# An encoder trunk on one core: boundary products doubled for six blocks instead of eight, a weight split moved behind the first gate, and the differential logits of a head in one burst

## The chip, the cores and the metric

One core of a Trainium2 chip runs the kernel. TensorE (PE) does the matmuls and transposes into PSUM, which has eight banks of 128 partitions; VectorE (DVE), ScalarE (ACT) and GpSimd (POOL) do the elementwise work; SyncE (SP) issues the loads of weights. The metric is the device time of one execution in microseconds; the kernel before takes 1092.3 us, the median of three runs.

## The reference, cut to what matters

A sequence of 16 meta tokens and 256 tokens (T = 272, D = 1024) goes through two layers. Each layer is a half-step SwiGLU feed-forward, a token mixer, and a second half-step feed-forward; every one of the six sub-layers has a norm at its input and one at its output. The mixer of layer 0 is a neighbourhood attention on a 4 x 64 grid, that of layer 1 a differential attention with a relative-position bias.

```
h = h + 0.5 * rmsnorm(swiglu(rmsnorm(h, g[0]), gate0, up0, down0), g[1])
h = h + rmsnorm(mixer(rmsnorm(h, g[2])), g[3])
h = h + 0.5 * rmsnorm(swiglu(rmsnorm(h, g[4]), gate1, up1, down1), g[5])
# mixer of layer 1, per head, with two half heads s = 0, 1 of width 64:
logits[s] = (q[s] * 64 ** -0.5) @ k[s].T + bias
a = softmax(logits[0]) - lam * softmax(logits[1])
o = rmsnorm(a @ v, subln_g) * (1 - lambda_init)
```

## The kernel before

**Weights and precision.** All activations are held transposed, 128 features on the partitions and 272 (or 256) tokens along the row, in eight blocks. The weights are 328 units of 1024 x 128, 512 KB each, loaded in order of use by SP into five `raw` buffers. Each value is split into a high and a low part of the type fp32r: `split_hi` (L128) casts half a unit on ACT to `whi`, `split_lo` (L134) subtracts on DVE to `wlo`; two of each make a unit ready, and the second `split_lo` issues the load that goes into the freed raw buffer. A **pump** splits one unit ahead of its use; with `W_BUFS` = 7, up to seven units may be split and not done. A product of one 128 x 128 block is three matmuls (`mm3`, L182 to L184): `whi` by the high part of the input, `wlo` by the high part, `whi` by the low part. A unit is eight blocks, 24 matmuls.

**Banks.** PSUM's eight banks are one `st` for statistics, three named `att`, and four named `acc`. The feed-forwards alternate over the seven (`all_banks`); in the attentions `acc` holds projections and `att` the rest.

**The norms.** The scale of an input norm (`r2`) is not applied to the input but to the product: the input's parts `xhi`, `xlo` are of h times the gain, and `r2` multiplies what comes out of PSUM. `InputRstd.begin` sums squares with single-column matmuls (L247), DVE adds the epsilon (`v`), POOL takes the power, `end` spreads the result over a bank by three transposes (L268), and ACT copies it to `r2` (L305).

**The start.** `start` has seven gate and up units of the first feed-forward: four in a group while the input arrives, then units 4, 5 and 6 one by one. The sums come in unit 5, the transposes ahead of unit 6's first block. Behind the last matmul `pump(4)` splits four units. Then the feed-forward reads the banks: `gt` (L437) and `ut` (L438) on DVE multiply gate and up by `r2`, ACT takes the silu, DVE the product.

**The boundaries.** A sub-layer's output f is added to h only after its own norm, whose scale is known when all eight blocks of f are there. `Post.feed` takes each block off PSUM: the square on ACT (added up on POOL, L278), f on DVE (`fg`), and f times the next gain split into `fhi` and `flo`. At each of the five boundaries between sub-layers `enter` then fills the wait: unit 0 of the next sub-layer is multiplied by the old h (`xhi`, `xlo`) into one bank `ab[0]` and by f (`fhi`, `flo`) into another, `ab[1]`, all eight blocks of both, 48 matmuls. In their midst stand the sums of f's squares (ahead of block `ready`, 6 or 7, of the first product) and the transposes that spread f's scale (ahead of block 2 of the second). `Post.add` scales f, adds it to h (L357) and makes the new `xhi` (L282) and `xlo`. `ab[1]` times the scale plus `ab[0]` is unit 0's result. `proj_group` then takes the next five units block by block, all high parts of a block first, then its low parts, with the sums of the new input norm ahead of block 6 and its transposes ahead of block 7.

**The order.** PE runs in program order everywhere. On DVE, ACT and POOL the feed-forwards run in program order too (`tc.manual_schedule()`); in the attentions a scheduler orders the three. There, a **filler** (`Filler`: the projections of units 6 to 23 and the first three output groups, 165 blocks of three matmuls) is cut into chunks by `pipeline`, and the steps of a head (the differential attention's are `logits`, `weights`, `turn_v`, `turn_a`, `values`, `scale`, `turn_o`) stand at set chunks, eight chunks a head. Pumps stand at three of every eight chunks. In the differential attention `logits` is called twice a head (chunks 2 and 3, one half of the queries each): three matmuls for each of the two half heads, which lie on partitions 0 to 63 and 64 to 127, into two `att` banks; DVE adds the bias and reduces (`tensor_tensor_reduce`), ACT takes exponentials (L1011). `weights` makes A of both half heads (L1019 on ACT, L1020 on DVE), and `turn_a` (chunks 7 and 8) transposes it on PE (L1079).

Of the kernel before, what the change touches and what calls it, by code (L numbers as in the profile page):

```python
# [39 lines left out]
W_BUFS = 7  # L40
# [9 lines left out]
def encoder_kernel(ctx, tc, xT, wall, gT, bqkvT, boT, sublnT, rpbP, metab, lam_p, rel,  # L50
# [20 lines left out]
    def att_tile():  # L71
        return psum.tile([P, 512], F32, tag="att", name=nm("att"), bufs=3)

    def acc_tile():

        pools["turn"] = (pools["turn"] + 1) % 7
        if pools["wide"] and pools["turn"] % 2:
            return att_tile()
        return psum.tile([P, 512], F32, tag="acc", name=nm("acc"), bufs=4)
# [115 lines left out]
    def proj_group(units, n_of, ihi, ilo, accs, hook):  # L195

        ws = [next_unit() for _ in units]
        for k in range(KB):
            if k in hook:
                hook[k]()  # L200
            for j in range(len(units)):
                n = n_of(units[j])
                nc.tensor.matmul(accs[j][:, :n], ws[j][0][:, k, :], ihi[:, k, :n], start=k == 0, stop=False)  # L203
                nc.tensor.matmul(accs[j][:, :n], ws[j][1][:, k, :], ihi[:, k, :n], start=False, stop=False)  # L204
            for j in range(len(units)):
                n = n_of(units[j])
                nc.tensor.matmul(accs[j][:, :n], ws[j][0][:, k, :], ilo[:, k, :n], start=False, stop=k == KB - 1)  # L207
        done(len(units))
# [79 lines left out]
    class InputRstd:  # L288
# [5 lines left out]
        def feed(self, m, engine=nc.gpsimd):  # L294
            sq = square(h[:, m, :self.n], self.n)
            self.acc = sq if m == 0 else add_squares(self.acc, sq, self.n, engine)
# [10 lines left out]
    class Post:  # L307
# [3 lines left out]
        def __init__(self, n, gain, bias, gain_next, n_next, ready):  # L311
            self.n, self.gain, self.bias = n, gain, bias
            self.gain_next, self.n_next, self.ready = gain_next, n_next, ready
            self.acc = None

        def open(self):
            self.cm = tc.tile_pool(name=nm("fx"), bufs=1, side="right")
            pool = self.cm.__enter__()
            self.fhi = pool.tile([P, KB, T], F32R, tag="fhi", name=nm("fhi"))
            self.flo = pool.tile([P, KB, T], F32R, tag="flo", name=nm("flo"))  # L320

        def feed(self, m, ps):
            n = self.n
            f = fg[:, m, :n]
            pump_hi() if m < KB - 1 else None
            if self.bias is None:
                sq = square(ps, n)
                nc.vector.tensor_scalar(out=f, in0=ps, scalar1=self.gain[:, m:m + 1], scalar2=None, op0=ALU.mult)
            else:
                sq = square(ps, n, bias=self.bias[:, m:m + 1])  # L330
                nc.vector.tensor_scalar(out=f, in0=ps, scalar1=self.bias[:, m:m + 1],
                                        scalar2=self.gain[:, m:m + 1], op0=ALU.add, op1=ALU.mult)
            self.acc = sq if m == 0 else add_squares(self.acc, sq, n)
# [29 lines left out]
    def enter(post, n_of, ab, rest):  # L363
# [5 lines left out]
        for k in range(KB):  # L369
            if k == post.ready:  # L370
                post.rstd()
# [828 lines left out]
```

## Time and profile before

| kernel before | us |
|---|---|
| median of three runs (1091.28 to 1093.07) | 1092.3 |
| the profiled execution, whole | 1092.72 |
| its span in the profile | 1090.9 |
| PE busy, share of the span | 99% |
| DVE busy, share of the span | 71% |
| ACT busy, share of the span | 56% |

The span runs from the first to the last instruction that the profiler recorded. Engines are busy side by side, so the shares add up to more than 100%. A wait in brackets behind an instruction, as in "[3.36 <-DVE gt L437]", is the engine's idle time ahead of it and what ended it. PEclk is the share of TensorE's full clock that was granted in a stretch. The matmul records overlap: a matmul's record lasts longer than the distance to the next one's start.

### The profile page before, as it was taken

The numbers are of one execution on the slowest core, as the hardware profiler recorded it, in microseconds if no ns is written. First come the engines' busy times: TensorE is split into PE (matmuls) and PEld (weight loads), VectorE is DVE, ScalarE is ACT, GpSimd is POOL, SyncE is SP. The second block draws the span as 40 slices with busy tenths as digits, with TensorE's granted clock in tenths as the row PEclk, the third lists the DMA queues.
The fourth block names the chain that finished last, engine by engine and source line by source line (L and its number), as shares of the span: only waits on it lengthen the run. The fifth ranks groups of instructions, "written<-read, shape, count | busy, mean of one in ns | idle before, by whom it ended". The sixth has DMA issues, their size and how long they took to land.

```text
span 1090.9 us, 22240 instructions
## 1 busy us (share of the span) xinstructions
PE 1076.9 (99%) x8482; PEld 1053.2 (97%) x8482; DVE 776.1 (71%) x1679; ACT 615.6 (56%) x1414; POOL 134.5 (12%) x259
## 2 busy tenths in 40 slices
PE   9899999999999999999999999999999999999997
PEld 8899999999999999999999999999999999999986
DVE  6876668687777896665578766666887778867642
ACT  6555455467666564445546544554677855655541
POOL 0000001143122260000130000001321131000000
PEclk9999999999999999999999999999999999999999
DMA  8599784615324375796526655555253344755541
GB/s 273 184 152 249 220 232 155 194 59 194 117 98 136 100 230 175 201 233 190 176 61 216 193 185 163 177 184 182 72 180 98 117 136 124 244 182 186 183 166 39
DMA packets 65772, 181.49 MB, mean 166 GB/s; under 512 B 13944, under 2 KB 23672, under 8 KB 65656
## 3 DMA queue, kind: packets, MB, share of 16 engines
q1 hardware_dynamic: 65232, 179.73, 54.4%
q8 instruction: 67, 1.10, 0.4%
q14 instruction: 41, 0.34, 0.1%
q10 hardware_dynamic: 432, 0.33, 0.1%
HBM read 178.91 MB, written 1.20 MB: 165 GB/s over the span
## 4 chain that ended last, share of the span: by engine, by line
PE 91%; DVE 4%; ACT 2%; issue 1%; POOL 0%; DMA 0%; POOLq 0%; ACTq 0%; DVEq 0%
PE acc L182 16%; PE acc L184 15%; PE acc L183 15%; PE att L182 10%; PE att L184 9%; PE att L183 9%; PE acc L204 1%; PE acc L203 1%; PE acc L207 1%; DVE wlo L134 1%; PE acc L513 1%; PE acc L512 1%; PE acc L511 1%; DVE h L357 1%; DVE xlo L285 1%
## 5 line engine op out<-in xcount | busy, mean ns | idle before, releaser
L134 DVE TENSOR_TENSOR wlo<-raw,whi 128x512 fp32r<-128x512 f32 (+2 forms) x668 | 437.2, 694 | 57.1 <-ACT whi L128 54.0
L128 ACT CAST whi<-raw 128x512 fp32r<-128x512 f32 (+2 forms) x668 | 374.9, 607 | 96.8 <-issue 43.5
L182 PE MATMUL acc<-xhi,whi 128*128 128x272 f32 (+1 forms) x1008 | 297.5, 295 | 3.4 <-DVE gt L437 3.4
L184 PE MATMUL acc<-xlo,whi 128*128 128x272 f32 (+1 forms) x1008 | 290.5, 288 | 0.0
L183 PE MATMUL acc<-xhi,wlo 128*128 128x272 f32 (+1 forms) x1008 | 289.6, 287 | 0.0
L182 PEld LDWEIGHTS acc<-xhi,whi 128*128 128x128 f32 x1008 | 190.8, 189 | 7.8 <-issue 6.3
L183 PEld LDWEIGHTS acc<-xhi,wlo 128*128 128x128 f32 x1008 | 190.9, 189 | 0.0
L184 PEld LDWEIGHTS acc<-xlo,whi 128*128 128x128 f32 x1008 | 190.7, 189 | 0.0
L182 PE MATMUL att<-xhi,whi 128*128 128x272 f32 (+1 forms) x552 | 158.8, 288 | 0.0
L184 PE MATMUL att<-xlo,whi 128*128 128x272 f32 (+1 forms) x552 | 158.7, 287 | 0.0
L183 PE MATMUL att<-xhi,wlo 128*128 128x272 f32 (+1 forms) x552 | 158.1, 286 | 0.0
L439 ACT ACTIVATE gt<-gt 128x272 f32<-128x272 f32 (+1 forms) x88 | 37.7, 428 | 142.4 <-DVE gt L437 142.4
L182 PEld LDWEIGHTS att<-xhi,whi 128*128 128x128 f32 x552 | 104.1, 189 | 0.0
L184 PEld LDWEIGHTS att<-xlo,whi 128*128 128x128 f32 x552 | 104.1, 189 | 0.0
L183 PEld LDWEIGHTS att<-xhi,wlo 128*128 128x128 f32 x552 | 104.0, 188 | 0.0
L184 PE MATMUL acc<-mlo,whi 128*128 128x272 f32 x286 | 82.9, 290 | 0.0
L183 PE MATMUL acc<-mhi,wlo 128*128 128x272 f32 x286 | 82.4, 288 | 0.0
L182 PE MATMUL acc<-mhi,whi 128*128 128x272 f32 x286 | 82.1, 287 | 0.0
L443 ACT CAST mhi<-ut 128x272 fp32r<-128x272 f32 (+1 forms) x88 | 36.5, 415 | 66.7 <-DVE ut L441 66.7
L184 PE MATMUL att<-mlo,whi 128*128 128x272 f32 x242 | 70.1, 290 | 0.0
L278 POOL TENSOR_TENSOR sqa<-sqa,sq 128x272 f32<-128x272 f32 (+1 forms) x60 | 50.3, 838 | 159.3 <-ACT sq L273 157.2
L183 PE MATMUL att<-mhi,wlo 128*128 128x272 f32 x242 | 69.7, 288 | 0.0
(241 smaller groups left out, 2018.9 us busy)
## 6 DMA issues: line engine op xcount, KB each, us to landing
raw<-wall SPq DMA_DIRECT2D x324, 512.0 KB, 4.1
bias<-tab SPq DMA_DIRECT2D x8, 320.0 KB, 8.2
raw<-wall SPq DMA_DIRECT2D x16, 128.0 KB, 3.8
bias<-tab SPq DMA_DIRECT2D x8, 256.0 KB, 8.4
h<-xT SPq DMA_DIRECT2D x3, 272.0 KB, 4.2
out<-ht SPq DMA_DIRECT2D x3, 256.0 KB, 2.0
grow<-glast SPq DMA_DIRECT2D x1, 512.0 KB, 5.1
h<-xT ACTq DMA_DIRECT2D x2, 136.0 KB, 4.3
```

Of the source, the lines that this page charges most:

```text
L128: nc.scalar.copy(split[i][0][:, sl], raw[i][:, sl])
L134: nc.vector.tensor_tensor(out=wlo[:, sl], in0=raw[i][:, sl], in1=whi[:, sl].bitcast(F32), op=ALU.subtract)
L182: nc.tensor.matmul(ps, whi_k, mhi, start=first, stop=False)
L183: nc.tensor.matmul(ps, wlo_k, mhi, start=False, stop=False)
L184: nc.tensor.matmul(ps, whi_k, mlo, start=False, stop=last)
L203: nc.tensor.matmul(accs[j][:, :n], ws[j][0][:, k, :], ihi[:, k, :n], start=k == 0, stop=False)
L204: nc.tensor.matmul(accs[j][:, :n], ws[j][1][:, k, :], ihi[:, k, :n], start=False, stop=False)
L207: nc.tensor.matmul(accs[j][:, :n], ws[j][0][:, k, :], ilo[:, k, :n], start=False, stop=k == KB - 1)
L278: engine.tensor_tensor(out=t[:, :n], in0=acc[:, :n], in1=sq[:, :n], op=ALU.add)
L285: nc.vector.scalar_tensor_tensor(out=xlo[:, m, :n], in0=h[:, m, :n], scalar=gain[:, m:m + 1], in1=xhi[:, m, :n].bitcast(F32), op0=ALU.mult ...
L439: nc.scalar.activation(gt[:, :n], gt[:, :n], AF.Silu)
L443: nc.scalar.copy(mhi[:, f, :n], ut[:, :n])
```

## The change

**Boundaries.** Unit 0 is multiplied twice for the first six blocks only (`AHEAD = 6`); its blocks 6 and 7 join `proj_group` and use the new `xhi` and `xlo`, in the bank `ab[0]`. So `fhi` and `flo` have six blocks, the sums of f's squares stand ahead of block 4 of the first product, the last square is added on DVE, and the order in `feed` changes for the last blocks. In `proj_group` the hooks stand behind a block's high parts instead of ahead of them. **Start.** The four pumps behind unit 6 are gone; the transposes stand ahead of block 7 of unit 5 instead of ahead of unit 6, with one pump ahead of them. The pumps in `evac` stay. **Banks and buffers.** Four `att` and three `acc` banks instead of three and four, eight weight buffers instead of seven; the DMA scratch shrinks. **Attentions.** `enter` and the staging of the first six units stand in `manual_schedule`. **Differential attention.** `logits` makes all twelve matmuls of a head at once, into four banks, alternating between the two half heads; chunks and pumps get new numbers, and the fillers are spread by `ahead`.

```diff
-W_BUFS = 7
+W_BUFS = 8
+AHEAD = 6
...
-        return psum.tile([P, 512], F32, tag="att", name=nm("att"), bufs=3)
+        return psum.tile([P, 512], F32, tag="att", name=nm("att"), bufs=4)
...
-        return psum.tile([P, 512], F32, tag="acc", name=nm("acc"), bufs=4)
+        return psum.tile([P, 512], F32, tag="acc", name=nm("acc"), bufs=3)
...
+    def proj_group(units, n_of, ihi, ilo, accs, hook, begun=()):
+        parts = [(w, acc, n, AHEAD) for w, acc, n in begun]
+        parts += [(next_unit(), acc, n_of(u), 0) for u, acc in zip(units, accs)]
         for k in range(KB):
+            here = [p for p in parts if k >= p[3]]
+            for w, acc, n, _ in here:
+                nc.tensor.matmul(acc[:, :n], w[0][:, k, :], ihi[:, k, :n], start=k == 0, stop=False)
+                nc.tensor.matmul(acc[:, :n], w[1][:, k, :], ihi[:, k, :n], start=False, stop=False)
             if k in hook:
                 hook[k]()
...
+            for w, acc, n, _ in here:
+                nc.tensor.matmul(acc[:, :n], w[0][:, k, :], ilo[:, k, :n], start=False, stop=k == KB - 1)
+        done(len(parts))
...
         def feed(self, m, ps):
...
+            if m == KB - 1:
+                self.acc = add_squares(self.acc, sq, n, nc.vector)
...
+            if m >= AHEAD:
+                pump_lo()
+                return
...
         n0 = n_of(0)
         w = next_unit()
-        for k in range(KB):
-            if k == post.ready:
+        for k in range(AHEAD):
+            if k == 4:
                 post.rstd()
-            mm3(ab[0][:, :n0], w[0][:, k, :], w[1][:, k, :], xhi[:, k, :n0], xlo[:, k, :n0], k == 0, k == KB - 1)
-        for k in range(KB):
+            mm3(ab[0][:, :n0], w[0][:, k, :], w[1][:, k, :], xhi[:, k, :n0], xlo[:, k, :n0], k == 0, False)
+        for k in range(AHEAD):
             if k == 2:
                 post.spread()
             mm3(ab[1][:, :n0], w[0][:, k, :], w[1][:, k, :], post.fhi[:, k, :n0], post.flo[:, k, :n0],
-                k == 0, k == KB - 1)
-        done()
+                k == 0, k == AHEAD - 1)
...
+        pump(1)
+        proj_group(range(1, 1 + len(rest)), n_of, xhi, xlo, rest, {6: ir.begin, 7: ir.end}, [(w, ab[0], n0)])
         nc.vector.tensor_tensor(out=u0[:, :n0], in0=ab[0][:, :n0], in1=u0[:, :n0], op=ALU.add)
-        pump(1)
-        proj_group(range(1, 1 + len(rest)), n_of, xhi, xlo, rest, {6: ir.begin, 7: ir.end})
-        pump(1)
         return [u0] + rest, ir
...
         proj_group(range(FIRST), lambda u: n, xhi, xlo, accs, {})
+
+        def end():
+            pump(1)
+            ir.end()
+
         for i in range(FIRST, 7):
-            proj(accs[i], n, xhi, xlo, {5: {2: ir.begin}, 6: {0: ir.end}}.get(i))
-        pump(4)
+            proj(accs[i], n, xhi, xlo, {5: {2: ir.begin, 7: end}}.get(i))
         return accs, ir
...
-            accs = [acc_tile() for _ in range(4)]
+            accs = [acc_tile() for _ in range(3)]
             ab = [att_tile() for _ in range(2)]
-            accs, ir = enter(before, nof, ab, accs + [att_tile()])
+            with tc.manual_schedule():
+                accs, ir = enter(before, nof, ab, accs + [att_tile(), att_tile()])
...
+                ps = [[att_tile() for _ in rows] for _ in range(2)]
+                for qt in range(2):
+                    q = slice(qt * P, (qt + 1) * P)
+                    for i, (a, b) in enumerate(((qhi, khi), (qlo, khi), (qhi, klo))):
+                        for s, r in enumerate(rows):
+                            nc.tensor.matmul(ps[qt][s][:, :T], a[r, q], b[r, :], start=i == 0, stop=i == 2)
...
-            at = [(2, logits, 0), (3, weights, 0), (3, logits, 1), (4, weights, 1), (7, turn_a, 0), (8, turn_a, 1)]
+            at = [(6, weights, 0), (7, weights, 1), (11, turn_a, 0), (12, turn_a, 1)]
             steps = [(c, lambda hh, go=go, qt=qt: go(hh, qt)) for c, go, qt in at]
-            steps += [(6, turn_v), (10, values), (11, scale), (13, turn_o)]
-            pipeline(fl, steps, (0, 5, 6))
+            steps += [(5, logits), (9, turn_v), (14, values), (15, scale), (18, turn_o)]
+            pipeline(fl, steps, (0, 1, 2), ahead=3)
...
-    nc = bacc.Bacc("TRN2", target_bir_lowering=False, num_devices=1)
+    nc = bacc.Bacc("TRN2", target_bir_lowering=False, num_devices=1, dynamic_dma_scratch_size=1024)
```

The changed order is shown at three places. In the rows, a name before the arrow is written, the names behind it are read, and numbers count tiles. First DVE at the first norm: `v` is the epsilon added to the sums, `gt` and `ut` the first gate and up block taken off PSUM. Before:

```order
L255 TENSOR_SCALAR v_404<-st_403 128x3
L134 TENSOR_TENSOR wlo_459<-raw_218,whi_458 128x512 x2
L134 TENSOR_TENSOR wlo_467<-raw_221,whi_466 128x512 x2
L134 TENSOR_TENSOR wlo_475<-raw_229,whi_474 128x512 x2
L134 TENSOR_TENSOR wlo_483<-raw_255,whi_482 128x512 x2
L437 TENSOR_TENSOR gt_498<-acc_135,r_27_432 128x272
L438 TENSOR_TENSOR ut_499<-att_136,r_27_432 128x272
L441 TENSOR_TENSOR ut_499<-gt_498,ut_499 128x272
L134 TENSOR_TENSOR wlo_504<-raw_275,whi_503 128x512 x2
L444 TENSOR_TENSOR mlo_494<-ut_499,mhi_493 128x272
```

And of the changed kernel:

```order
L135 TENSOR_TENSOR wlo_270<-raw_215,whi_269 128x512 x2
L257 TENSOR_SCALAR v_404<-st_403 128x3
L135 TENSOR_TENSOR wlo_427<-raw_218,whi_426 128x512 x2
L452 TENSOR_TENSOR gt_474<-att_135,r_27_437 128x272
L453 TENSOR_TENSOR ut_475<-acc_136,r_27_437 128x272
L456 TENSOR_TENSOR ut_475<-gt_474,ut_475 128x272
L135 TENSOR_TENSOR wlo_480<-raw_221,whi_479 128x512 x2
L459 TENSOR_TENSOR mlo_470<-ut_475,mhi_469 128x272
```

Between `v` and the first `gt` stood eight weight splits, of four units; now two stand there, and the next two come after the product `ut`.

Second, PE at the logits of the first head; `acc` is the filler. Before, the first of its two bursts:

```order
L184 MATMUL acc_10242<-xlo,whi_10153 128x272
L182 MATMUL att_10257<-hi_10187,hi_10181 128x272
L183 MATMUL att_10257<-hi_10187,lo_10182 128x272
L184 MATMUL att_10257<-lo_10188,hi_10181 128x272
L182 MATMUL att_10263<-hi_10187,hi_10181 128x272
L183 MATMUL att_10263<-hi_10187,lo_10182 128x272
L184 MATMUL att_10263<-lo_10188,hi_10181 128x272
L182 MATMUL acc_10242<-xhi,whi_10153 128x272
```

And of the changed kernel, the one burst:

```order
L1034 MATMUL att_10263<-hi_10141,hi_10136 128x272
L1034 MATMUL att_10264<-hi_10141,hi_10136 128x272
L1034 MATMUL att_10263<-hi_10141,lo_10137 128x272
L1034 MATMUL att_10264<-hi_10141,lo_10137 128x272
L1034 MATMUL att_10263<-lo_10142,hi_10136 128x272
L1034 MATMUL att_10264<-lo_10142,hi_10136 128x272
L1034 MATMUL att_10265<-hi_10141,hi_10136 128x272
L1034 MATMUL att_10266<-hi_10141,hi_10136 128x272
L1034 MATMUL att_10265<-hi_10141,lo_10137 128x272
L1034 MATMUL att_10266<-hi_10141,lo_10137 128x272
L1034 MATMUL att_10265<-lo_10142,hi_10136 128x272
L1034 MATMUL att_10266<-lo_10142,hi_10136 128x272
```

The six matmuls that wrote one bank after the other have become twelve that alternate between two banks, and then between the next two.

Third, ACT at the start of the differential attention, from the copy of `r2` on: `hi` are high parts of q and k, L1011 (L1042 in the changed kernel) the first exponentials. Before:

```order
L305 COPY r_712_10136<-st_10110 128x272
L990 CAST hi_10181<-qk_10179 128x256
L128 CAST whi_10238<-raw_9782 128x512 x2
L128 CAST whi_10325<-raw_9812 128x512 x2
L990 CAST hi_10187<-qk_10185 128x272
L128 CAST whi_10346<-raw_9844 128x512 x2
L128 CAST whi_10385<-raw_10018 128x512 x2
L990 CAST hi_10195<-qk_10193 128x256
L128 CAST whi_10492<-raw_10159 128x512
L1011 ACTIVATE L_10253,sm_10256<-L_10253,nmx_10255 128x272 x2
```

And of the changed kernel, where the copy of `r2` and two more `hi` stand ahead of the first row:

```order
L1013 CAST hi_10150<-qk_10148 128x256
L1013 CAST hi_10155<-qk_10153 128x272
L129 CAST whi_10162<-raw_9708 128x512 x2
L1013 CAST hi_10198<-qk_10196 128x256
L129 CAST whi_10202<-raw_9751 128x512 x2
L129 CAST whi_10217<-raw_9778 128x512 x2
L129 CAST whi_10231<-raw_9810 128x512 x2
L129 CAST whi_10329<-raw_9971 128x512 x2
L129 CAST whi_10350<-raw_10168 128x512 x2
L1013 CAST hi_10253<-qk_10251 128x272
L1042 ACTIVATE L_10261,sm_10280<-L_10261,nmx_10279 128x272 x2
L1042 ACTIVATE L_10261,sm_10286<-L_10261,nmx_10285 128x272 x2
```

Of the `whi` casts nine half units stood ahead of the first exponentials; now twelve do, and four casts of q and k stand in a row ahead of them.

## Rows read from the trace of the kernel before

**Rows 1.** The page's busy times: us, share of the span, instructions.

```profile
PE 1076.9 (99%) x8482; PEld 1053.2 (97%) x8482; DVE 776.1 (71%) x1679; ACT 615.6 (56%) x1414; POOL 134.5 (12%) x259
```

**Rows 2.** Windows: length; PE, PEld, DVE, ACT, POOL busy (instructions); clock; DMA; GB/s.

```profile
32.60:36.00 3.40, 3.40 (x15) 3.40 (x16) 3.18 (x7) 2.63 (x6) 0.00 (x0) 0.50 1.02 349
...
36.00:39.40 3.40, 3.40 (x28) 3.40 (x28) 3.18 (x8) 1.79 (x4) 0.00 (x0) 1.00 0.88 313
...
100.00:140.00 40.00, 40.00 (x319) 40.00 (x319) 26.52 (x53) 20.25 (x42) 0.00 (x0) 1.00 0.83 236
...
1000.00:1020.00 20.00, 20.00 (x171) 20.00 (x171) 14.32 (x30) 9.96 (x22) 0.00 (x0) 1.00 0.55 179
```

**Rows 3.** Waits of PE: waiting instruction, releaser: us in total, times, longest.

```profile
PE acc L182 <- DVE gt L437: 3.4, 1, 3.4
...
PE st L247 <- POOL sqa L278: 1.3, 3, 0.6
...
PE att L1079 <- DVE A L1020: 1.0, 1, 1.0
```

**Rows 4.** Timeline at the first norm: start, duration, instruction, [wait, releaser]; PE, ACT, DVE.

```profile
28.87 0.29 PE L184 MATMUL att<-xlo,whi 128*128 128x272 f32 x1
...
32.52 0.53 PE L182 MATMUL acc<-xhi,whi 128*128 128x272 f32 x1 [3.36 <-DVE gt L437]
...
26.18 0.39 ACT L305 COPY r<-st 128x272 f32<-128x272 f32 x1 [4.20 <-PE st L268]
...
27.11 4.90 DVE L134 TENSOR_TENSOR wlo<-raw,whi 128x512 fp32r<-128x512 f32 x8 [3.35 <-ACT whi L128]
...
31.94 0.43 DVE L437 TENSOR_TENSOR gt<-acc,r 128x272 f32<-128x272 f32 x1
```

**Rows 5.** Timeline at the entries of two sub-layers, PE and ACT.

```profile
349.12 0.83 PE L247 MATMUL st<-ones,sqa 128*128 128x1 f32 x6 [0.38 <-POOL sqa L278]
...
351.14 0.54 PE L268 MATMUL st<-ident,r 128*128 128x128 f32 x3
...
352.73 0.53 ACT L282 ACTIVATE xhi<-h,g_sb 128x272 fp32r<-128x272 f32 x1 [3.38 <-DVE h L357]
...
908.76 0.61 PE L247 MATMUL st<-ones,sqa 128*128 128x1 f32 x4 [0.60 <-POOL sqa L278]
```

**Rows 6.** Timeline of PE around two bursts of differential logits.

```profile
782.48 0.29 PE L184 MATMUL acc<-xlo,whi 128*128 128x272 f32 x1
...
783.28 0.39 PE L182 MATMUL acc<-xhi,whi 128*128 128x272 f32 x1
...
783.51 0.29 PE L183 MATMUL acc<-xhi,wlo 128*128 128x272 f32 x1
...
784.01 0.29 PE L184 MATMUL acc<-xlo,whi 128*128 128x272 f32 x1
...
785.07 0.39 PE L182 MATMUL acc<-xhi,whi 128*128 128x272 f32 x1
```

**Rows 7.** Start of the differential attention: timeline (PE, ACT), DMA issues, a window.

```profile
776.84 0.49 PE L268 MATMUL st<-ident,r 128*128 128x128 f32 x3
...
781.18 0.41 ACT L990 CAST hi<-qk 128x272 fp32r<-128x272 f32 x1
...
781.50 2.18 ACT L128 CAST whi<-raw 128x512 fp32r<-128x512 f32 x4
...
784.92 0.51 ACT L1011 ACTIVATE L<-L,nmx 128x272 f32<-128x272 f32 x1
...
788.78 0.28 PE L184 MATMUL acc<-xlo,whi 128*128 128x272 f32 x1
...
790.07 0.44 PE L1079 MATMUL att<-ident,A 128*128 128x128 f32 x2 [1.01 <-DVE A L1020]
...
raw<-wall SPq DMA_DIRECT2D x324, 512.0 KB, 4.1
...
783.00:871.00 88.00, 86.99 (x710) 81.65 (x707) 71.70 (x211) 72.03 (x226) 17.58 (x21) 1.00 0.41 136
```

More of the change, by code (lines that the diff above doesn't have):

```diff
@@ L868, in natten @@
                     single.append((i, lambda p=pairs, go=go: go(p)))
-            for u in range(6):
-                stage(u, accs[u])
-            post = Post(T, gains(l, 3), bo_sb, gain_next, n_next, 7)
+            with tc.manual_schedule():
+                for u in range(6):
+                    stage(u, accs[u])
+                pump(1)
+            post = Post(T, gains(l, 3), bo_sb, gain_next, n_next)
             fl = Filler(range(6, 24), lambda u: T, stage, ohi, olo, post)
@@ L933, in pipeline @@
             want = total * (i + 1) // chunks_all
+            if ahead:
+                even = total * (last + ahead) // chunks_all
+                want = (even * (i + 1) // last if i < last else
+                        even + (total - even) * (i + 1 - last) // (chunks_all - last))
             fl.fill(want - filled)
@@ new lines, in stage_hi, with stage, logits @@
+                return lambda: engine.tensor_tensor(out=lo, in0=s, in1=hi.bitcast(F32), op=ALU.subtract)
+            def stage(u, a):
+                low = stage_hi(u, a)
+                if low is not None:
+                    low()
+            def logits(hh):
+                (qhi, qlo), (khi, klo) = staged[3 * hh], staged[3 * hh + 1]
+                L = cur["L"] = pt.tile([P, 2, 2, T], F32, tag="L", name=nm("L"))
+                cur["A"] = pt.tile([P, 2, T], F32, tag="A", name=nm("A"))
+                rows = [slice(64 * s, 64 * s + 64) for s in range(2)]
+                ps = [[att_tile() for _ in rows] for _ in range(2)]
[4 more added lines that the diff above has]
+                            nc.tensor.matmul(ps[qt][s][:, :T], a[r, q], b[r, :], start=i == 0, stop=i == 2)
+                for qt in range(2):
+                    nmx = pt.tile([P, 2], F32, tag="nmx", name=nm("nmx"))
+                    sm = pt.tile([P, 2], F32, tag="sm", name=nm("sm"))
+                    for s in range(2):
+                        nc.vector.tensor_tensor_reduce(
+                            out=L[:, qt, s, :], in0=ps[qt][s][:, :T], in1=b4[:, hh, qt, :], scale=-1.0, scalar=3e38,
+                            op0=ALU.add, op1=ALU.min, accum_out=nmx[:, s:s + 1])
+                        nc.scalar.activation(L[:, qt, s, :], L[:, qt, s, :], AF.Exp, bias=nmx[:, s:s + 1],
+                                             scale=-1.0, accum_out=sm[:, s:s + 1])
+                    cur["sm", qt] = sm
```

105 lines of the change are left out of this document (44 added, 61 removed).

## The prediction

> **What bounds the kernel now.** Read first the busy times of the page [rows 1]: PE is busy for 1076.9 of 1090.9 us, so whatever leaves the time must leave PE's own queue: matmuls that are no longer issued, or stretches in which it issues none. A busy PE here means a matmul started every 0.125 us: 40 us hold 319 matmuls of 272 columns, 20 us hold 171 of 256 columns, 0.117 us each [rows 2]. These are the prices used below; the 0.29 us of one matmul's record is its latency, not its cost. Second, read who PE waited for [rows 3]: 3.4 us for one `gt`, 1.3 us for sums of squares, 1.0 us for a softmax weight A. That view counts from the end of the last matmul's record, 0.16 us late (0.29 - 0.125), so starts are used here: a gap is the distance between two starts less 0.125. [...]
>
> **The first norm.** PE's last matmul before the gap starts at 28.87, the next at 32.52: 3.52 us lost, ended by `gt` on DVE at 31.94 [rows 4]. r2 was there at 26.57 (ACT's copy, 26.18 + 0.39); what DVE did between was 4.90 us of eight weight splits [rows 4], the four pump(1). The changed order leaves two of the eight, and they come ahead of r2: ACT converts that unit while it waits for PE's transposes (idle 4.20 us there), and DVE has 3.35 us idle [rows 4]. The transposes also move up by three matmuls (0.38 us). So `gt` follows r2 at about 26.2, 2.4 us before PE has finished unit 6, and the gap goes: -3.52. The splits that moved are late only if PE asks for them: unit 8 is needed one unit (24 x 0.125 = 3.0 us) after 29.0, and DVE has it by 28.8 (0.35 + 0.35 + 0.35 for `gt`, `ut` and the product, with ACT's silu between, then 1.2 for the split). With the gap gone the clock should not fall: 28 - 15 = 13 matmuls, -1.6 us [rows 2]. Together -5.1 (at the least -3.0 if a gap of half a microsecond and some clock loss stay).
>
> **The doubled blocks.** At each of five entries two blocks of three matmuls fewer: 18 matmuls of 272 columns and 12 of 256, 18 x 0.125 + 12 x 0.117 = 3.7 us. These are on PE, the engine that bounds, so they count in full unless a wait takes their place. -3.7.
>
> **Waits at the entries.** Four go. The sums of the sandwich norm after the first attention wait 0.38 + 0.16 = 0.54 for POOL's addition, at 349.12 [rows 5]: the changed kernel asks for them 9 matmuls (1.1 us) earlier, but DVE then adds the last square in 0.35 (a `gt` of that size, next start less start) where POOL needs over twice that, without two fhi/flo pairs ahead of it (ACT's fhi of block 6 stands ahead of the last square in the old order); by hand, both come within 0.1 us. The sums of the input norms wait 0.60 + 0.16 at 908.76 [rows 5], 0.28 + 0.16 in the third wait of that line [rows 3], and some 0.2 in one that this count just misses; they now come 12 matmuls later relative to the block's other work, behind the hi halves, so 1.5 us cover 0.8. In all -1.9. Two new ones come. After the spread (transposes at 351.14) DVE scales and adds, and ACT has written the first xhi at 352.73 + 0.53 = 353.26 [rows 5]: 2.1 us. PE fills that now with 12 matmuls and the transposes, 1.85 us, where it had 18: 0.25 at each of five entries. And unit 0's bank is now read by DVE only after the group's last lo matmuls; the next unit, which takes that bank, waits about 0.1 each. +1.4 after rounding down. Net -0.5. In the two attentions one bank less is left for accumulators: the third output group takes the bank of the last v, 0.75 us behind it, and may wait for its staging, 0 to 0.7 each like the waits just named; the staging in program order gives the first logits of the first attention their k earlier by as much. Net 0.
>
> **The differential logits.** In the old kernel a head's logits come in two bursts. Where both halves find their banks, the two row groups run together: starts in pairs, the filler before at 782.48, the one behind at 783.28 and its second matmul at 783.51, so 0.68 + 0.10 = 0.78 us over the filler's own pace. The next burst, where the second bank is late, costs 784.01 to 785.07, 0.93 + 0.10 = 1.04 [rows 6]. A head costs between 1.56 and 1.82, eight heads 12.5 to 14.6. One burst of twelve has the same two changes of shape and three more pairs: 0.78 + 3 x 0.125 = 1.16, 9.3 in all. Gain 3.2 to 5.3, less what four banks at once may wait for; I take 4.0.
>
> Its price is at the start of that attention. PE now meets the first `turn_a` wait with 1.17 us (788.78 to 790.07 less 0.12) [rows 7]. Count both kernels from the transposes of the input norm (776.84, the old kernel). Old: PE is there after 21 filler blocks, at +11.9, and A is there at +13.1. New: 30 filler blocks (14 of 256 columns, 4.9 us; 16 of 272, 6.0), a burst of 1.16 and the v transposes 0.33, from the first filler at +1.2: PE is there at +13.6. But the order puts six units of whi ahead of the first exponentials on ACT, where four and a half stood. A unit is 1.09 us (2.18 for two), a hi cast 0.32 (781.18 to 781.50) [rows 7]: with six casts from +2.0 on, 8.5 us, +10.5. The sixth unit's raw buffer is that of the first, so its load is issued only when DVE has split the first (+7.1), and takes 4.1 us [rows 7]: whi from +11.4 to +12.5, a hi cast, then four exponentials of 0.51 from +12.8 to +14.9 [rows 7]; copies of v, half a unit, A's scaling and DVE's product are some 1.8 (an estimate, 0.55 for the half unit and 0.3 to 0.45 for each of the others, like the casts): +16.6. PE waits 3.0 instead of 1.17: +1.8 (bounds -1.2, if ACT is not held up, and +4, with a load that comes late). Net of the logits -2.2.
>
> **What costs nothing.** The eighth weight buffer: one more unit may be split ahead, and PE waits for splits in no large gap [rows 3]. [...] The last product's early part is one unit shorter, its matmul count the same; the tail after PE is untouched.
>
> **The sum.** -5.1 - 3.7 - 0.5 - 2.2 = -11.5. The profiled execution took 1092.72 us (span 1090.9 and 1.8 around it), 0.4 over the median of 1092.3. 1092.7 - 11.5 = 1081.2, on the median's side 1080.8; I say 1081.0.
>
> **Rivals.** (a) *No new wait at the differential start, full logits.* If the exponentials come before PE needs A, -3.0, and the burst gives its 5.3 instead of 4.0: 1081.0 - 4.3 = 1076.7. For it: PE has 1.7 us more of filler ahead of the first `turn_a`. Against it: six units of whi on ACT in the order. (b) *The attention waits more.* The wait at the first `turn_a` reaches 3.5 us like the one at the start, and the clock falls as it did there, 1.6 [rows 2, 4]; the four banks cost 0.4 in each of eight heads, 3.2, and the entries 0.5 more: 1081.0 + 0.5 + 1.6 + 3.2 + 0.5 = 1086.8. [...] (c) *The first norm does not give.* If unit 7's whi is not ready while ACT waits, because its load is late, the old gap stays: 1081.0 + 5.1 = 1086.1; against it: in the old trace the splits of that unit and the next three run on DVE without a pause [rows 4]. (d) *Slower.* The burst takes all four banks, and the next that need one (values, v) must wait for DVE's four reductions (0.36 each) behind a pump's wlo (1.2 a unit, three units pumped in a row). At 2.5 us a head, 20 us less the 4.0 counted as gain stand against the 7.5 of the rest: 1092.3 - 11.5 + 20 = 1100.8; it decides from 11.5 / 8 = 1.4 us a head. For it: DVE is busy 71.7 of 88 us there, ACT 72.0 [rows 7]. [...] Against it: the next user comes a chunk (two filler blocks, 0.8 us) later, and A has six chunks where it had five.
>
> **How the numbers follow.** Forecast 0.53, (a) 0.2, (b) and (c) 0.22 together, (d) 0.05. The range reaches from (a) to (b): 1076 to 1087. A measurement of this kernel tells some 0.2%, 2.2 us, from no change; every case but (d) lies below 1090.1, so faster 0.93, within 0.03 (waits that eat the gain halfway), slower 0.04.
>
> **What would show it.** PE: no gap after unit 6, and a granted clock of 1.00 from 10 us on. 30 matmuls fewer. No wait of PE for POOL's squares; some 0.25 us at the group's first xhi. One burst of twelve at about 1.2 a head. The largest wait of PE at the first `turn_a` of the differential attention, 2 to 4 us, released by DVE's A. Wrong: PE waiting for a bank or a reduction in every head, or waiting for wlo near 32 us.

## The result and the profile after

The changed kernel takes 1088.17 us (median of 5 runs, 1085.85 to 1088.28), the kernel before in the same comparison 1092.54 (5 runs). The ratio is 0.9949, with an interval of 0.9938 to 0.9960. It is faster, but by 4 to 7 us (the interval of the ratio) and not by 11.5, and it lies 1.2 us above the range of the prediction.

The page's busy times of the changed kernel, against [rows 1], and the longest waits of PE in it (in total, times, longest), against [rows 3]:

```profile
PE 1071.4 (99%) x8452; PEld 1047.4 (96%) x8452; DVE 770.8 (71%) x1669; ACT 606.2 (56%) x1394; POOL 127.0 (12%) x249
```

```profile
PE att L1110 <- DVE A L1051: 3.0, 1, 3.0
...
PE att L1082 <- DVE ob L1074: 1.0, 2, 0.7
PE st L249 <- DVE sqa L280: 0.7, 2, 0.5
PE att L804 <- DVE L L782: 0.7, 1, 0.7
PE att L1034 <- POOL lo L1016: 0.6, 1, 0.6
```

PE issues 30 matmuls fewer, and the 3.4 us for `gt` are gone. In their place stand 3.0 us for the first softmax weight A (1.0 before) and a row of waits of up to 0.7 us each: for `ob` (the scaled output of a head) and `lo` in the differential attention, for the last square `sqa`, and for the first softmax weights of the neighbourhood attention (L804).

The program is the same in every stage but for the places of a few matmuls, so the kernels can be laid side by side by PE's own marks: the transposes that spread a norm's scale, and the sums of squares. "By counts" is what the changed number of matmuls between two marks makes at 0.125 us (0.117 for 256 columns); "left" is the rest, gaps and clock.

| stage, between marks on PE (us) | before | after | change | by counts | left |
|---|---|---|---|---|---|
| first weight matmul to first transposes | 20.36 | 20.62 | +0.26 | -0.38 | +0.64 |
| first feed-forward, to the sums of its output | 189.00 | 183.52 | -5.48 | -0.38 | -5.1 |
| five entries, sums of f to transposes of the input norm | 92.66 | 99.44 | +6.78 | +6.3 | +0.5 |
| neighbourhood attention | 115.83 | 114.03 | -1.80 | -2.25 | +0.45 |
| second and third feed-forward | 371.36 | 368.04 | -3.32 | -3.7 | +0.4 |
| differential attention | 116.62 | 116.86 | +0.24 | -2.2 | +2.4 |
| last feed-forward | 172.99 | 172.17 | -0.82 | -1.05 | +0.2 |

The changes add up to -4.1. The first feed-forward gave its 5.1 us to the tenth. The loss against the forecast is in the differential attention, where -2.2 was forecast beside the counts and +2.4 came, and in small amounts at the entries, the neighbourhood attention and the feed-forwards. The +0.64 of the first row is no wider than what the loading varies between kernels with the same start (last section).

**The start.** Timeline of DVE and windows (columns as in [rows 2]) of the changed kernel, against [rows 4] and [rows 2]:

```profile
26.64 0.44 DVE L452 TENSOR_TENSOR gt<-att,r 128x272 f32<-128x272 f32 x1 [1.25 <-ACT r L309]
...
28.08 1.29 DVE L135 TENSOR_TENSOR wlo<-raw,whi 128x512 fp32r<-128x512 f32 x2
```

```profile
28.00:31.00 3.00, 3.00 (x26) 3.00 (x25) 2.94 (x7) 1.94 (x5) 0.00 (x0) 1.00 0.56 184
31.00:34.00 3.00, 3.00 (x26) 3.00 (x26) 2.77 (x7) 2.68 (x6) 0.00 (x0) 1.00 0.86 276
```

`gt` stands right behind r2, at 26.64 instead of 31.94, PE has no gap, and the clock stays at 1.00.

**The entries.** Timeline of PE and ACT at the first entry, where the group of five units begins:

```profile
213.10 0.28 PE L185 MATMUL att<-flo,whi 128*128 128x272 f32 x1
213.49 0.39 PE L204 MATMUL acc<-xhi,whi 128*128 128x272 f32 x1
```

```profile
212.92 0.52 ACT L284 ACTIVATE xhi<-h,g_sb 128x272 fp32r<-128x272 f32 x1 [4.56 <-DVE h L369]
```

The last product with f starts at 213.10, the first with the new h at 213.49, behind an `xhi` that is written at 213.44: 0.27 us over the pace, and 0.10 more for the matmul behind it. All five entries have this, at 0.37 to 0.46 us; it was 0.00 before.

**The differential attention.** Timeline at its start, PE, DVE and ACT, against [rows 7], and the window behind the first transposes of A:

```profile
789.33 0.44 PE L1110 MATMUL att<-ident,A 128*128 128x128 f32 x2 [2.96 <-DVE A L1051]
```

```profile
778.15 5.51 DVE L135 TENSOR_TENSOR wlo<-raw,whi 128x512 fp32r<-128x512 f32 x8
783.59 0.42 DVE L1010 TENSOR_TENSOR qk<-acc,r 128x272 f32<-128x272 f32 x1
783.94 0.42 DVE L1039 CUSTOM_DVE_ANT_0 L<-att,bias 128x272 f32<-128x272 f32 x1
```

```profile
783.83 1.14 ACT L129 CAST whi<-raw 128x512 fp32r<-128x512 f32 x2 [0.91 <-DMA raw<-wall]
784.87 0.42 ACT L1013 CAST hi<-qk 128x272 fp32r<-128x272 f32 x1
785.19 0.52 ACT L1042 ACTIVATE L<-L,nmx 128x272 f32<-128x272 f32 x1
```

```profile
791.30:793.30 2.00, 2.00 (x11) 1.75 (x10) 1.84 (x4) 2.00 (x7) 1.07 (x1) 0.50 0.89 262
```

PE had finished the logits at 780.65, but DVE split four units (eight halves) before it reduced them at 783.94, and ACT's exponentials came at 785.19, behind the sixth unit, whose load was 0.91 late. The exponentials follow the cast ahead of them without a wait, so ACT's queue set their time, and not the reductions. PE stood still for 3.1 us and then ran at half clock: 11 matmuls in 2 us where 16 fit at 0.125 us each.

What stands between the fillers (the projections that fill PE's time) in this attention adds up as follows, in us over the fillers' own pace, all eight heads:

| | before | after |
|---|---|---|
| logits | 13.75 | 10.79 |
| transposes of A | 6.54 | 8.80 |
| transposes of the output | 2.15 | 3.68 |
| transposes of v and values | 13.54 | 13.98 |
| fillers slower than their pace | 0.03 | 1.19 |

### The profile page after: what moved, and what is told of

Its sections match the earlier page's. It is cut to its first block, busy times and chain, and to the rows that moved or that the text cites. A ratio compares the mean times of both kernels' runs of the same rounds, so it can differ in the third digit from the quotient of the medians.

```text
span 1086.5 us, 22222 instructions
## 1 busy us (share of the span) xinstructions
PE 1071.4 (99%) x8452; PEld 1047.4 (96%) x8452; DVE 770.8 (71%) x1669; ACT 606.2 (56%) x1394; POOL 127.0 (12%) x249
## 4 chain that ended last, share of the span: by engine, by line
PE 89%; DVE 4%; issue 2%; ACT 2%; DMA 2%; POOL 0%; ACTq 0%; SPq 0%; POOLq 0%; DVEq 0%
PE acc L183 12%; PE acc L185 12%; PE att L183 12%; PE acc L184 12%; PE att L185 12%; PE att L184 12%; DVE wlo L135 2%; PE att L204 1%; PE att L209 1%; PE att L205 1%; DMA raw<-wall 1%; PE acc L204 1%; PE acc L205 1%; PE acc L209 1%; PE att L527 1%
## 5 line engine op out<-in xcount | busy, mean ns | idle before, releaser
L183 PE MATMUL acc<-xhi,whi 128*128 128x272 f32 (+1 forms) x792 | 234.5, 296 | 0.0
L185 PE MATMUL acc<-xlo,whi 128*128 128x272 f32 (+1 forms) x792 | 228.1, 288 | 0.0
L184 PE MATMUL acc<-xhi,wlo 128*128 128x272 f32 (+1 forms) x792 | 227.3, 287 | 0.0
L183 PE MATMUL att<-xhi,whi 128*128 128x272 f32 (+1 forms) x758 | 218.5, 288 | 0.0
L185 PE MATMUL att<-xlo,whi 128*128 128x272 f32 (+1 forms) x758 | 217.8, 287 | 0.0
L184 PE MATMUL att<-xhi,wlo 128*128 128x272 f32 (+1 forms) x758 | 216.9, 286 | 0.0
L183 PEld LDWEIGHTS acc<-xhi,whi 128*128 128x128 f32 x792 | 149.7, 189 | 3.2 <-issue 1.7
L184 PEld LDWEIGHTS acc<-xhi,wlo 128*128 128x128 f32 x792 | 149.8, 189 | 0.0
L185 PEld LDWEIGHTS acc<-xlo,whi 128*128 128x128 f32 x792 | 149.6, 189 | 0.0
L183 PE MATMUL att<-mhi,whi 128*128 128x272 f32 x286 | 82.1, 287 | 0.0
```

What stands on the lines that cost most here:

```text
L183: nc.tensor.matmul(ps, whi_k, mhi, start=first, stop=False)
L184: nc.tensor.matmul(ps, wlo_k, mhi, start=False, stop=False)
L185: nc.tensor.matmul(ps, whi_k, mlo, start=False, stop=last)
```

## The experiments

All were made from the changed kernel. Where a stage's length is named, it is that of the table above.

**The start alone undone.**

```
-            proj(accs[i], n, xhi, xlo, {5: {2: ir.begin, 7: end}}.get(i))
+            proj(accs[i], n, xhi, xlo, {5: {2: ir.begin}, 6: {0: ir.end}}.get(i))
+        pump(4)
```

> The changed kernel with the old start alone: the transposes ahead of unit 6 again, and four pumps behind it. Theory 1 (the start gained what was predicted, the loss lies elsewhere): the gap of 3.5 us and the half clock behind it come back, 1088.2 + 5.1 = 1093.3, with a granted clock of 0.50 right behind the gap. Theory 2 (the start gave only part of it, since the loading phase ahead of it, 0.4 us longer in the changed kernel's trace, is part of the change): about 1092.5 and no more.

Measured 1093.16 us, 0.9998 (0.9989 to 1.0007) of the kernel before. Its waits of PE and the window behind the gap:

```profile
PE att L183 <- DVE gt L453: 3.4, 1, 3.4
```

```profile
32.40:36.00 3.60, 3.38 (x16) 3.41 (x17) 3.38 (x8) 2.82 (x6) 0.00 (x0) 0.56 0.97 328
```

Theory 1 holds: gap and half clock are back, the first feed-forward is 188.05 us long instead of 183.52 (and by its marks has three matmuls fewer, so 4.9 us come back), and with it goes the whole gain. All else in the change together is worth nothing measurable.

**Six, seven and eight doubled blocks.**

```
-AHEAD = 6
+AHEAD = 8
...
-        proj_group(range(1, 1 + len(rest)), n_of, xhi, xlo, rest, {6: ir.begin, 7: ir.end}, [(w, ab[0], n0)])
+        proj_group(range(1, 1 + len(rest)), n_of, xhi, xlo, rest, {6: ir.begin, 7: ir.end})
+        done()
```

So with eight blocks unit 0 no longer takes part in the group of the next five units.

> The changed kernel with all eight blocks of unit 0 multiplied twice again (30 matmuls more, 3.7 us), the rest as changed. Theory 1 (from the trace of the changed kernel: PE waits about 0.37 us for the first new high part at each of five entries because the cover is six matmuls shorter): those waits, 1.9 us in all, go, and 1088.2 + 3.7 - 1.9 = 1090.0. Theory 2 (the waits have another cause, and the 30 matmuls count in full): 1091.9.

Measured 1089.35 us, 0.9956 (0.9942 to 0.9969). From the first transposes to PE's last matmul it is 1.62 us longer than the changed kernel, near theory 1's 1.8: of the 3.7 us of matmuls removed, 2.1 come back as waits. The gap ahead of the first `xhi` is 0.00 at all five entries.

> The changed kernel with seven blocks of unit 0 multiplied twice instead of six: 15 matmuls more, 1.85 us, of which three at each entry lie behind the transposes that spread f's scale. Theory 1 (the wait of 0.37 us for the first new high part comes from cover that is three matmuls short): the wait is 0.0 to 0.1 at all five, and from the sums of the first input norm to the end the kernel is within 0.4 us of the changed one. Theory 2 (the first high part moves back with the matmuls ahead of it): the waits stay, and it is 1.85 us longer.

Measured with `AHEAD = 7` (unit 0's last block in the group): one run of 1090.01 us; by the same two marks, 1.76 us longer than the changed kernel. Neither theory fits. The gap at the first `xhi` is gone, as theory 1 said, but the time isn't gained. PE's timeline in this kernel at the sums of the first entry's input norm:

```profile
226.39 0.29 PE L205 MATMUL att<-xhi,wlo 128*128 128x272 f32 x1
226.90 0.47 PE L249 MATMUL st<-ones,sqa 128*128 128x1 f32 x3 [0.23 <-DVE u L395]
```

The sums now wait 0.39 us (226.39 to 226.90 less a matmul) for DVE's `u`, which reads the spread scale last (it lies in the bank `st` that the sums want) and stands behind the additions of all eight blocks on DVE. Three entries have this wait, the differential entry 0.51, the last none. From the transposes that spread f's scale to these sums it is 15.2 us with eight blocks (212.85 to 228.07), 15.15 with seven and 15.1 with six: with eight PE's own matmuls fill it, with seven a wait stands at its end, with six one at its start. Taking away the first block (eight to seven) gained nothing; the second (seven to six) gained 1.76 of its 1.85. The wait at the sums explains most of the first, but not all: with eight blocks each of the three later feed-forwards is also 0.3 us shorter (the second 183.77 us, against 184.06 with seven and with six), as one matmul fewer stands in it and the next unit no longer waits 0.18 us for unit 0's bank.

**The old logits.** The two bursts (the old function `logits`, left out here), the old chunks and pumps in place of the new:

```
...
-            steps += [(5, logits), (9, turn_v), (14, values), (15, scale), (18, turn_o)]
-            pipeline(fl, steps, (0, 1, 2), ahead=3)
+            at = [(2, logits, 0), (3, weights, 0), (3, logits, 1), (4, weights, 1), (7, turn_a, 0), (8, turn_a, 1)]
+            steps += [(6, turn_v), (10, values), (11, scale), (13, turn_o)]
+            pipeline(fl, steps, (0, 5, 6))
```

> The changed kernel with the old differential logits: two bursts a head, the old chunks and pumps (weights at 3 and 4, transposes of A at 7 and 8, pumps at 0, 5 and 6), fillers spread evenly. Theory 1 (the new plan lost more in waits than its burst gained): the bursts cost 3.0 us more, the waits at the transposes of A, of the output and at the banks, some 5 us, go: 1088.2 + 3.0 - 5.4 = 1085.8. Theory 2 (the prediction's sum, -2.2 for burst and new wait together): 1090.4.

Measured 1088.44 us, 0.9951 (0.9939 to 0.9964), the stage 116.52 us, 0.3 shorter, and the entry behind it 0.55 longer. Neither theory: burst and plan are worth nothing on balance. But the old logits did not bring back the old stage either, which without other losses would be 116.62 - 2.2 = 114.4. Another 2 us were lost to some other part of the change.

**The scheduler's entries.**

```
-            with tc.manual_schedule():
-                accs, ir = enter(before, nof, ab, accs + [att_tile(), att_tile()])
+            accs, ir = enter(before, nof, ab, accs + [att_tile(), att_tile()])
```

and likewise for the staging and in the neighbourhood attention.

> The changed kernel with the entries and the staging of the two attentions left to the scheduler again instead of program order. Theory 1 (program order of the entries is worth little): within 0.5 us of 1088.2. Theory 2 (program order there causes the waits at the first transposes of the neighbourhood attention, 1.2 us, and the sums of the differential entry, 0.2): 1086.8. Theory 3 (it is what makes the staging early enough): 1090 or more.

Measured 1086.54 us, 0.9940 (0.9927 to 0.9952): theory 2 in size, but not at its places. The entries got 0.5 longer in all; the differential attention fell from 116.86 to 114.91. ACT's timeline at its start in this kernel:

```profile
772.80 0.39 ACT L309 COPY r<-st 128x272 f32<-128x272 f32 x1 [6.86 <-PE st L270]
773.08 1.66 ACT L129 CAST whi<-raw 128x512 fp32r<-128x512 f32 x3
...
784.07 0.52 ACT L1039 ACTIVATE L<-L,nmx 128x272 f32<-128x272 f32 x1
```

The scheduler puts three half units of `whi` ahead of the first staging; in program order ACT waits there for DVE's `qk` (1.06 and 1.42 us idle) and casts the first half unit at 777.03. So the exponentials come 1.1 us earlier, counted from the transposes of the input norm, PE waits 1.69 us for A instead of 3.12, and the clock stays at 1.00. The part of the change that I had put down as neutral cost 1.7 to 2.0 us in this stage (which took 116.64 and 116.86 us in two traces of the changed kernel); from the first transposes to PE's last matmul it cost 1.35.

> The changed kernel with the old differential logits and the old plan, and with the entry and the staging of the differential attention left to the scheduler; read by the length of that stage, from the transposes of its input norm to the sums of its own output norm: 116.6 us before, of which the change takes 2.25 away by counts (114.4 with no other gain or loss), 116.9 in the changed kernel, 116.5 with the old logits alone, 114.9 with the scheduler's entry alone. Theory 1 (program order at the entry costs some 2 us, and the burst gains nothing on balance): 114.4 to 114.9. Theory 2 (the four and three banks cost the old logits as much): 116 or more. Theory 3 (the burst is worth its 3 us once the entry is the scheduler's): 117.5.

Measured: one run of 1086.71 us, the stage 115.52, between theories 1 and 2. With the scheduler's entry the burst is thus worth 0.6 (115.52 against 114.91). The old logits are 1.0 slower in program order (116.52 against 115.52), but PE's wait for A is 2.28 us in both; behind it the clock fell to 0.50 in the one and stayed at 1.00 in the other, and that program order brings this about is not shown.

**Pumps after the first softmax.**

```
+            now = (0, 6, 7) if ahead and i < 8 else pumps
-            if i % 8 in pumps:
+            if i % 8 in now:
```

> The changed kernel with two of the three pumps of the first eight chunks of the differential attention moved from chunks 1 and 2 to chunks 6 and 7, so that three and a half units of whi stand ahead of the first exponentials on ACT and two and a half of wlo ahead of the first reductions on DVE, instead of six and four. Theory 1 (the weight splits ahead of the first softmax hold up A): the wait of 3.0 us at the first transposes of A goes, and that stage is 113.9 us long instead of 116.9. Theory 2 (A is late for another reason, or another wait takes its place, such as PE for the splits that are now late): 116 or more.

Measured: one run of 1086.21 us, the stage 114.34 us, 2.5 shorter. DVE's timeline at the first reductions, and PE's waits in this stage:

```profile
778.07 3.10 DVE L135 TENSOR_TENSOR wlo<-raw,whi 128x512 fp32r<-128x512 f32 x4
...
782.05 0.43 DVE L1040 CUSTOM_DVE_ANT_0 L<-att,bias 128x272 f32<-128x272 f32 x1
```

```profile
PE att L1083 <- DVE ob L1075: 0.8, 2, 0.5
PE att L1111 <- DVE A L1052: 0.7, 1, 0.7
PE att L1035 <- POOL lo L1017: 0.6, 1, 0.6
```

Theory 1 holds: the weight splits ahead of the first softmax were what held A up. The gap falls from 3.12 to 0.87, the clock stays at 1.00, and the reductions come at 782.05. The edit moves the casts on ACT and the splits on DVE together, so it does not tell the two apart. The entry that follows is 0.5 longer, so 2.0 remain.

> The late pumps of the differential attention together with its entry and staging left to the scheduler, which casts three half units of whi while ACT waits for r2. Theory 1 (late pumps and the scheduler's entry take away the same wait for A): the stage is between 114.0 and 114.9 us, no better than with either alone (114.3, 114.9). Theory 2 (they take away different waits): 113 or less.

Measured: one run of 1087.63 us, the stage 115.78, in neither range and worse than with either alone. The gap ahead of A is 1.35, and a wait of 1.6 us for `ob` in the second head took the place of the rest. The two remedies don't add up; that the scheduler then finds another order is the likely reason, not a shown one.

**Where the waits for `ob` come from.** In the changed kernel the values of a head stand one chunk behind the logits of the next. ACT, POOL and DVE ahead of one such wait:

```profile
806.73 1.16 ACT L1050 ACTIVATE A<-L,sm 128x272 f32<-128x272 f32 x2
807.80 0.26 ACT L1065 ACTIVATE jk<-att 128x128 f32<-128x128 f32 x1
```

```profile
810.25 0.70 POOL L1068 TENSOR_TENSOR ss<-ss,mhalf 128x2 f32<-128x2 f32 x1
```

```profile
810.99 0.42 DVE L1074 TENSOR_TENSOR ob<-att,ss 128x256 f32<-128x256 f32 x1 [1.41 <-POOL ss L1068]
```

The squares of the values (L1065, 807.80) queue on ACT behind four exponentials (from 804.69 on) and A, and the second of them (808.56) behind half a unit of `whi` as well; the power on POOL stands behind a `lo` (809.55, 0.74 us), and PE's transposes wait until 811.47. The steps one chunk earlier put the squares first:

```
-            at = [(6, weights, 0), (7, weights, 1), (11, turn_a, 0), (12, turn_a, 1)]
-            steps += [(5, logits), (9, turn_v), (14, values), (15, scale), (18, turn_o)]
+            at = [(6, weights, 0), (7, weights, 1), (10, turn_a, 0), (11, turn_a, 1)]
+            steps += [(5, logits), (9, turn_v), (13, values), (14, scale), (17, turn_o)]
```

> The changed kernel with the transposes of A, the values, the scaling and the transposes of the output one chunk earlier (10, 11, 13, 14, 17), so that a head's values stand ahead of the next head's logits in the same chunk, and its squares ahead of the four exponentials on ACT. Theory 1 (the waits for ob come from squares queued behind the exponentials of the next head): the waits at the transposes of the output, 1.5 us, go; the first transposes of A wait one chunk longer, 0.8: the stage is 116.2 us. Theory 2 (values now wait for the copies of the transposed A, 0.3 a head): 118 or more.

Measured: one run of 1096.73 us, the stage 122.23. Every wait for `ob` is gone, which fits theory 1 as to their cause, though the `whi` and the `lo` in that chain moved too and are not told apart from the exponentials. PE's waits show what took their place:

```profile
PE att L1034 <- DVE nmx L1039: 3.8, 7, 0.9
PE att L1110 <- DVE A L1051: 3.4, 1, 3.4
```

The values hold one of the four banks until they are scaled, and the burst right behind them wants all four: between its third and its fourth bank PE waits until the burst's own first reduction frees one, 3.8 us in seven heads by the first line, up to 0.9 in one. It is the shortage of rival (d), though the burst waits and not the next user. In the changed kernel, where the values come a chunk later, PE has no such wait.

Not all of the 8.6 us over the changed kernel are this. The stage is 5.4 longer, and part of that is the clock, which stays at 0.50 behind the first A until 797.3 (until 793.9 in the changed kernel). Some 2.6 arose at the start, which the edit does not touch: the loading took 1.7 us longer, and the clock read 0.50 from 25.9 to 29.3 us.

> Both of the two above: the late pumps and the steps one chunk earlier. Theory 1: the stage is 112.4 to 113.2 us long (3.0 and 1.5 less than 116.9, up to 0.8 of a wait left at the first A). Theory 2: either of them turns into another wait, 115 or more.

Measured: one run of 1089.85 us, the stage 117.14, theory 2. The first gap falls to 1.58 and the clock stays at 1.00; the seven waits of the bursts remain (3.7 us). So at full clock the earlier values cost 2.8 us net (117.14 against 114.34 with the late pumps alone).

**Late pumps, and the output's transposes one chunk later.**

```
-            steps += [(5, logits), (9, turn_v), (14, values), (15, scale), (18, turn_o)]
+            steps += [(5, logits), (9, turn_v), (14, values), (15, scale), (19, turn_o)]
```

> The late pumps, and the transposes of the output one chunk later (19 instead of 18), which leaves the order on ACT as it is but gives the squares, the power on POOL and the scaling 0.8 us more. Theory 1 (PE waits for ob because the squares stand behind the next head's exponentials): 1.5 of the 1.8 us of those waits go, the stage is 112.8 us instead of 114.3, and the whole is some 3.5 us under the changed kernel, at a ratio of 0.992 to the kernel before. Theory 2 (the scaling holds a bank, and the next logits wait for it in place of PE's transposes): 114.3 or more.

Measured 1085.59 us, 0.9930 (0.9918 to 0.9942); the changed kernel beside it 0.9953. It beats both kernels, the changed one by 2.75 us. The stage is 114.30 us, no shorter than with the late pumps alone, so theory 2 is right here; the entry behind it is back at 18.45. PE's waits:

```profile
PE att L1095 <- DVE vs L1002: 1.5, 1, 1.5
...
PE att L1035 <- ACT ptb L1114: 0.6, 1, 0.6
PE att L1061 <- DVE nmx L1040: 0.6, 1, 0.6
```

None for `ob`; others of the same size, for banks and for v, in their place.

> The changed kernel once more, beside the run above and on the same chip. Theory 1 (all but the loading of the input and of the first units takes the same time in every execution): every stage from the sums of the first input norm on is within 0.1 us of its earlier trace, the differential attention within 0.4, and the ratio is within 0.993 to 0.997. Theory 2 (its runs spread because the later stages vary): stages differ by more than that.

Measured 1088.34 us, 0.9953 (0.9941 to 0.9965). Theory 1 holds but for a hundredth: all stages behind the first transposes lie within 0.11 us of the first trace, the differential attention within 0.22.

## Why the prediction was off

The largest miss is the term "Net of the logits -2.2": +2.4 was found, 4.6 us worse. The entries with the feed-forwards behind them missed by 1.6, the neighbourhood attention by 0.45.

**The start: right.** -5.1 forecast, -5.1 found, and 4.9 when undone. (The clock of the kernel before also read 0.50 from 1087.4 us on; PE had issued its last matmul at 1084.1, so it cost nothing.)

**The doubled blocks and the waits at the entries: the term was mis-sized.** The matmuls count 3.7 as said. Net of the waits -4.2 was forecast; by the table the entries and the three later feed-forwards, where the next unit waits 0.18 us for unit 0's bank, left +1.1 over the counts: about -2.6. The step that failed is the pair "-1.9, +1.4". The wait at the first `xhi` was 0.37 to 0.46 at each entry where 0.25 stood; the sums after the first attention still wait 0.35 us of their 0.54; the differential entry has a new 0.2 at its sums. So about 1.5 of the 1.9 went, and some 2.8 came where 1.4 stood. I had priced each wait by its own cover; in the run with seven blocks the wait covered at one end of the entry (0.00 at the first `xhi`) came back at the other (0.39 at the sums of the first entry).

**The neighbourhood attention: "net 0" was +0.45.** The first logits lost their wait, as said; the first transposes of the weights (L804) took it over, 0.85 and 0.35 more than in the other heads.

**The differential logits: the sign was wrong, by three steps.** First, the burst was mis-sized: 1.15 us a head in five of eight as computed, but 0.2 to 0.96 more in three, one of them at half clock and one behind a `lo` on POOL: 3.0 gained instead of 4.0. Second, the wait at the first `turn_a`: forecast 3.0, found 3.1, for the reason named (the sum's "+7.1" and 4.1 make +11.2 and not +11.4; the cast came at +11.6). But the sum left out a fall of the clock, which I had kept for rival (b): it read 0.50 behind this wait, as at the start behind 3.5 us [rows 2, 4]. It costs some 1.6 us (0.33 at the second transposes, 0.47 at the next logits, the rest in the fillers). At A it read 0.50 behind every gap measured from 2.82 to 3.52 us (last section). Third, the outputs: 1.5 us of waits for `ob`, which no term had. The step that moved ahead queued its four exponentials on ACT (from 804.69 on in the head shown) ahead of the other's squares (807.80); I followed the burst to its banks and to A, and not to the squares behind.

**The rivals.** (b) is what happened in kind: half clock behind the first A, and more at the entries; its four banks at 0.4 a head were too dear in the changed kernel. (a), (c) and (d) did not happen, (d) only in an experiment that moved the values.

**What I took for nothing.** Program order at the entries of the attentions stood in the sum only as an advantage for k. It kept ACT from using its idle time (1.06 and 1.42 us), and cost 1.7 to 2.0 us in the differential attention. The eighth weight buffer, also taken for nothing, and the split of the banks into four and three were not tried by themselves.

## What to carry over

When independent work (here weight splits) may be hoisted, ask what it is hoisted in front of: here an ordered stretch that left ACT idle for 1.06 and 1.42 us pushed that work behind it, in front of the first urgent step. The wait of 3.12 us on PE had two prices here, its length and the clock of 0.50 behind it, some 1.6 us; write both in the sum, not one in a rival. Two marks that one chain on another engine connects should be costed as one interval: here it took 15.1 to 15.2 us with six, seven and eight blocks, and covering one end of it (0.37 to 0.00 us at the first entry) brought a wait of 0.39 at the other.

## What the runs showed of the hardware

The granted clock behind the first transposes of A, by PE's gap ahead of them: 1.00 behind 0.87, 1.17, 1.35, 1.58 and 1.69 us, 0.50 at the latest 2 us behind 2.82, 2.86, 3.12 and 3.52. At 2.28 us it was both: 0.50 with the old logits in program order, 1.00 with them under the scheduler. Windows of the one and the other:

```profile
787.20:789.20 2.00, 2.00 (x11) 2.00 (x10) 1.36 (x3) 1.70 (x6) 0.00 (x0) 0.50 0.55 186
```

```profile
787.40:789.40 2.00, 2.00 (x19) 2.00 (x19) 2.00 (x5) 1.70 (x5) 0.00 (x0) 1.00 0.85 326
```

What tells the two apart was not tried. Nor was every shorter gap free: in the run with the values first, the clock read 0.50 from 25.9 us on behind a gap of 1.41 us at the first sums, PE's longest since the first weight matmul (17 matmuls in the next 3.4 us, 29 in the 3.4 behind them); the clock's mean was 0.993 over that run and 0.997 over the changed kernel's.

In the kernel before, matmuls on partitions 0 to 63 and 64 to 127 overlapped even where one product of three is written behind the other. PE started them in pairs, the two of the first pair in 0.40 us where one such record takes 0.39, and the pairs 0.24 and 0.12 us apart:

```profile
782.69 0.40 PE L182 MATMUL att<-hi,hi 64*128 64x272 f32 x2
782.93 0.30 PE L183 MATMUL att<-hi,lo 64*128 64x272 f32 x2
783.05 0.29 PE L184 MATMUL att<-lo,hi 64*128 64x272 f32 x2
```

The feed-forwards behind an entry repeated to a few hundredths of a microsecond: the second took 184.06 to 184.08 us in all the traces of changed kernels with six or seven doubled blocks. The differential attention differed by 0.2 between two traces of the changed kernel. What varied most is the time from the first weight matmul to the first transposes, while the input and the first units are loaded: 20.0 to 22.2 us in the kernels that do the same there. That spread is as wide as that of the runs of one kernel (1085.85 to 1088.28 for the changed one), so effects of half a microsecond can be read here from stages, and not from whole times.
